# Loads of attention values and compressed keys held back by a one-column write that needs a unit's softmax sum

## The chip, the cores and the metric

The kernel is one program on one core of a Trainium2 chip. The metric is device time in microseconds (us). Before the change the median of 3 runs is 2306.26 us (2304.66 to 2307.88). The profile comes from a further, profiled execution, which took 2301.17 us.

The engines are named as the profile names them: PE (TensorE, matmuls), PEld (its weight loads), DVE (VectorE), ACT (ScalarE), POOL (GpSimd), SP (SyncE, which issues every DMA of this kernel). Each engine works through its instructions in the order in which they stand.

## The reference

The reference is one step of a two-layer encoder on 1024 prompt frames and 64 sample frames, which the kernel handles as 1088 columns of width 1024. Cut to what matters, each layer does this:

```
h = rmsnorm(x);  z = h @ w_in                      # split into the inputs and gates of three mixers
o_a = mla_attend(...) * silu(g_a)                  # 8 heads; keys and values from a compressed ckv
o_b = pool_mix(...) * silu(g_b)                    # trailing means
o_c = ca_attend(...) * silu(g_c)                   # 4 "chunk" heads: own chunk and 8 before it, with a bias
m = gates_a * (o_a @ w_o_mla) + gates_b * (o_b @ w_o_pool) + gates_c * (o_c @ w_o_ca)
x = x + m @ w_out
x = x + sigmoid(rmsnorm(x) @ w_ple_gate) * (ple @ w_ple_proj)
```

For the compressed attention the values of all heads come from one matrix, `v = ckv_all @ w_ukv[:, values]`, where `ckv_all` has 128 features and 1600 columns (1024 prompt, 512 cached, 64 sample).

## The kernel before

Every layer runs as: projections (GEMMs), the attention phase, a merge, the output GEMM, the PLE gate GEMM. Values in float32 are split into a high and a low part (`split`, lines 108 and 119), and products are three matmuls (`mm3`, lines 130 to 132). Large intermediates live in DRAM between the stages.

**Units.** The attention phase (`attn_phase`) takes the 4 chunk heads and then the 8 compressed ("latent") heads one after another. A head has nine units, one for each block of 128 queries; for a chunk head they come in the order `QC` = sample block first, then blocks 0 to 7. Unit i: `scores` on PE with a DVE pass that adds the bias and takes the minimum (chunk heads, L984 and L986), `exp` on ACT (L807), the reciprocal of the sum on DVE (L814), the scaling of the probabilities P on POOL (L815). Two units later they are transposed (pT, L841) and split into PT, and then multiplied by the values V (pv, L867 for the sample block, L875 for a pair of blocks).

**Loads.** `ahead_of` is called by each unit's `scores`: at the second unit of head p it writes the loads of head p+1's Q, K and bias, at the sixth its values (`load_values`). A chunk head's V is one load of 128x1664 (`vc`); there are three V buffers. For the first latent head `values` loads the compressed keys into `ckf` (three pieces: 1024, 512 and 64 columns) and their weights into `wv`, then makes V from them (vps, L1024).

**Background.** Between the units the PLE projection runs (`ple_proj`): 16 steps, each of two blocks of six matmuls (pps), each block copied out of PSUM by ACT (L1394, tile `o`, two buffers), each step stored to DRAM (`pp<-o`). A step can write `o` only when the store of two steps before has landed. `pool_branch` (pu, pa, pb, pbm) and `merge_bc` (wbc, mps, of, g) follow the same manner.

**Order.** The code fixes what depends on what. The order on each engine is then made by the tile layer's scheduler, which places instructions by priority and by its own estimate of when their operands are there (`schedule_with_timeline_sim`). A load whose buffer is free and whose source is written can thus be placed on SP far ahead of its place in the code, and a new dependence moves instructions on every engine. All DMAs are on SP's one hardware queue; a DMA waits on SP for what it depends on and for the completion of an earlier DMA whose semaphore it takes over (there are eight of these), and what is behind it on SP waits with it.

Of the kernel before, what the change touches and what calls it, by code (L numbers as in the profile page):

```python
# [10 lines left out]
F32 = mybir.dt.float32  # L11
# [3 lines left out]
ALU = mybir.AluOpType  # L15
# [8 lines left out]
KT = 1600  # L24
# [49 lines left out]
class K:  # L74
# [382 lines left out]
    def w_pairs(self, l, begin):  # L457
# [129 lines left out]
        def done(k):  # L587
            a, b = z.pop(k), z.pop(k + 1)
            if k == Z_HQ:
                for j, t in enumerate((a, b)):  # L590
                    self.st(zd[k + j], t)
                self.tasks.append(stat(a, b))
            elif k == Z_CKV:
                def dst1(i, t):
                    self.st(d["ckv"][l], t)

                def dst2(i, t):
                    self.st(d["krope"][l], t[64:96])
                    store_hl(t, keydst(self.kr_d[l], slice(0, 32)), slice(64, 96))
                self.tasks.append(norm([a], S_128, 1, G_KV, dst1))  # L600
                self.tasks.append(norm([b], S_QH, 2, G_KR, dst2))
            elif k in (Z_QC, Z_KC):
                for j, t in enumerate((a, b)):
                    def dst(_, t, j=j):
                        if k == Z_KC:
                            self.st(d["cak"][l][j], t)
                            store_hl(t, keydst(self.kc_d[l][j]))
                        else:
                            store_hl(t, [(self.qc_d[l][j, 0], self.qc_d[l][j, 1], slice(0, T))])
                    self.tasks.append(norm([t], S_64, 2, G_CQ if k == Z_QC else G_CK, dst))  # L610
            else:
                for j, t in enumerate((a, b)):
                    if k == Z_VC:
                        self.st(d["cav"][l][j], t)
                        self.tasks.append(values(j, t))
                    else:
                        self.st(zd[k + j], t)
# [178 lines left out]
    def softmax(self, u, s, n, nb, st):  # L796

        nc = self.nc
        if not hasattr(u, "p"):
            u.p = self.sp.tile([128, 1024], F32, tag="P", name="P", bufs=NP)  # L800
        w = n // len(s)
        if nb == 2:
            nc.vector.tensor_tensor(st[:, 0:1], st[:, 0:1], st[:, 1:2], op=ALU.min)

        def exp():
            for c, x in enumerate(s):
                nc.scalar.activation(u.p[:, c * w:c * w + w], x, AF.Exp, bias=st[:, 0:1], scale=-1.0,  # L807
                                     accum_out=st[:, 2 + c:3 + c])
        u.exp = exp

        def norm():
            if len(s) == 2:
                nc.vector.tensor_add(st[:, 2:3], st[:, 2:3], st[:, 3:4])
            nc.vector.reciprocal(st[:, 4:5], st[:, 2:3])  # L814
            nc.gpsimd.tensor_scalar(u.p[:, :n], u.p[:, :n], st[:, 4:5], 1.0, op0=ALU.mult, op1=ALU.mult)  # L815
        u.norm = norm

# [97 lines left out]
    def load_values(self, p):  # L915
        if p < len(self.seq) and self.seq[p] not in self.vt:
            kind, h = self.seq[p]
            if kind == "c":
                v = self.vt[kind, h] = self.new_v().rearrange("p (b c) -> p b c", b=13)
                self.ld(v, self.vc_d[self.l][h])  # L920
            else:
                self.values(self.l, h)

    def new_v(self, dt=F32R):
        return self.sp.tile([128, 1664], dt, tag="V", name="V", bufs=NV)

    def ahead_of(self, p, qb):

        if qb == QC[0] and p == 0:
            self.load_values(0)  # L930
        order = QC if self.seq[p][0] == "c" else QM
        if qb == order[L1]:
            self.load_head(p + 1)
        if qb == order[L2]:
            self.load_values(p + 1)

    def out_of(self, kind, h):

        k = kind, h // 2
        if k not in self.ot:  # L940
            self.ot[k] = self.sp.tile([128, T], F32, tag="o", name="o", bufs=2)
        return self.ot[k]
# [50 lines left out]
    def load_latent(self, h, *t):  # L993
# [6 lines left out]
                self.ld(x[64:96], self.kr_d[l][n - 2])  # L1000
        return t

    def values(self, l, h):

        nc, sp = self.nc, self.sp
        if h == 0:
            self.ckf = self.at("ckf", KT, "ckf", F32)
            self.ld(self.ckf[:, :1024], self.d["ckv"][l][:, :1024])
            self.ld(self.ckf[:, 1024:1536], self.d["ckv_c"][l])
            self.ld(self.ckf[:, 1536:], self.d["ckv"][l][:, 1024:])  # L1010
            self.wv = self.at("wv", 512, "wv", F32)
            self.ld(self.wv, self.d["wukv"][l][:, 512:])
        vs = []
        for i in range(2):
            v = self.new_v().rearrange("p (b c) -> p b c", b=13)
            nc.gpsimd.memset(v[0:64, 12].bitcast(F32), 0.0)
            self.vt["m", h + i] = v
            vs.append(v)
        for b0 in range(0, 13, 4):
            nb = min(4, 13 - b0)  # L1020
            ps = self.pv.tile([128, 4, 128], F32, tag="v", name="vps")
            for b in range(nb):
                c0 = min((b0 + b) * 128, KT - 128)
                nc.tensor.matmul(ps[:, b], lhsT=self.ckf[:, c0:c0 + 128], rhs=self.wv[:, h * 64:(h + 2) * 64],  # L1024
                                 start=True, stop=True)
            p0 = 64 if b0 == 12 else 0
            for i, v in enumerate(vs):
                v = v[p0:, b0:b0 + nb]
                self.split(ps[p0:, :nb, 64 * i:64 * i + 64], v[:, :, :64], v[:, :, 64:])
# [603 lines left out]
```

## Time and profile before

| | |
|---|---|
| median of 3 runs | 2306.26 us |
| profiled execution | 2301.17 us |
| its span | 2299.2 us, 44770 instructions |
| busy share: PE, PEld, DVE, ACT, POOL | 94%, 90%, 80%, 53%, 30% |
| DMA: SP's queue, share of 16 engines' span | 53.9%, 382.95 MB in 221972 packets |
| chain that ended last | PE 63%, DVE 14%, DMA 12%, issue 3%, ACT 3%, POOL 2%, SPq 1% |

PE is busy nearly everywhere. In the page's 40 slices of 57.5 us each the DMA share is highest in the slice from 575 us (9 tenths) and just behind 1725 us, which is where the attention phase of each layer begins; PE's busy digit and its granted clock dip near there too. The phase of the first layer begins at about 560 us and that of the second at about 1700 us.

The time outside the span is 2301.17 - 2299.2 = 1.97 us.

### The profile page before, as it was taken

To read this page: it belongs to the slowest core of one execution; us is meant where nothing else is said; L and a number is where in the kernel's file an instruction comes from. 1 tells how busy PE (TensorE), PEld (TensorE's weight loads), DVE (VectorE), ACT (ScalarE), POOL (GpSimd) and SP (SyncE) were. 2 spreads that over 40 slices of the span, in tenths; PEclk is the share of its full clock that TensorE was granted. 3 is DMA by queue.
4 is the path that set the end of the run, shared out by engine and by line. 5 is a ranking of instruction groups with operands and counts; after the bars stand their busy time and mean duration, and the time that the engine had idled before them with its cause. 6 is when DMAs were issued, how large, how long until landed. Compare 5 with 4: busy or idle time off the path is not lost.

```text
span 2299.2 us, 44770 instructions
## 1 busy us (share of the span) xinstructions
PE 2160.5 (94%) x16134; PEld 2077.4 (90%) x16134; DVE 1838.5 (80%) x3750; ACT 1211.6 (53%) x2549; POOL 694.0 (30%) x918
## 2 busy tenths in 40 slices
PE   5999999999789999998979999999988899999988
PEld 4999999999688999998969999999987789999988
DVE  8677887675678888989997778877746788889898
ACT  6334355554676666445553343555546766654452
POOL 0000044666456553000000001547563565430000
PEclk8999999999899999998979999999999999999989
DMA  3534546355976764454634354544469766645354
GB/s 128 181 110 138 191 147 187 119 157 171 266 203 173 199 170 163 164 193 144 211 105 148 117 170 167 171 142 146 151 178 268 202 179 187 187 156 190 140 160 135
DMA packets 222192, 385.81 MB, mean 168 GB/s; under 512 B 30404, under 2 KB 114196, under 8 KB 221972
## 3 DMA queue, kind: packets, MB, share of 16 engines
q1 hardware_dynamic: 221972, 382.95, 53.9%
q8 instruction: 129, 2.11, 0.4%
q14 instruction: 91, 0.75, 0.1%
HBM read 248.16 MB, written 134.70 MB: 167 GB/s over the span
## 4 chain that ended last, share of the span: by engine, by line
PE 63%; DVE 14%; DMA 12%; issue 3%; ACT 3%; POOL 2%; SPq 1%; POOLq 0%; DVEq 0%; ACTq 0%
PE g L366 41%; PE S L1055 4%; PE pv L875 3%; PE pT L841 3%; DMA pp<-o 3%; DMA K<-bias_p 1%; PE mps L130 1%; DVE wop L119 1%; DMA r<-rd 1%; PE mps L132 1%; PE mps L131 1%; SPq L85 1%; DMA Q<-qc 1%; PE vps L1024 1%; DMA g<-z 1%
## 5 line engine op out<-in xcount | busy, mean ns | idle before, releaser
L108 ACT CAST wop<-wraw 128x512 fp32r<-128x512 f32 (+1 forms) x230 | 139.0, 606 | 266.7 <-PE g L366 180.0
L108 ACT CAST wop<-S 128x512 fp32r<-128x512 f32 x234 | 144.5, 619 | 154.0 <-PE g L366 146.6
L119 DVE TENSOR_TENSOR wop<-S,wop 128x512 fp32r<-128x512 f32 x210 | 163.9, 780 | 66.3 <-ACT wop L108 65.9
L815 POOL TENSOR_SCALAR P<-P,st 128x640 f32<-128x640 f32 (+8 forms) x216 | 156.0, 727 | 200.9 <-DVE st L814 128.6
L119 POOL TENSOR_TENSOR wop<-wraw,wop 128x512 fp32r<-128x512 f32 (+1 forms) x80 | 98.8, 1237 | 381.4 <-ACT wop L108 377.2
L119 DVE TENSOR_TENSOR PT<-pT,PT 128x512 fp32r<-128x512 f32 (+4 forms) x360 | 167.8, 474 | 43.1 <-ACT PT L108 41.1
L366 PE MATMUL g<-B11h,wop 128*128 128x272 f32 x960 | 175.5, 294 | 18.3 <-ACT B11h L110 12.3
L366 PE MATMUL g<-T3h,wop 128*128 128x272 f32 x960 | 178.2, 294 | 12.4 <-ACT T3h L108 11.9
L366 PE MATMUL g<-B21h,wop 128*128 128x272 f32 x960 | 180.6, 299 | 4.2 <-ACT P L378 4.1
L366 PE MATMUL g<-T2h,wop 128*128 128x272 f32 x960 | 177.6, 295 | 5.4 <-ACT T2h L108 5.3
L366 PE MATMUL g<-T1h,wop 128*128 128x272 f32 x960 | 176.1, 295 | 3.5 <-DVE z L629 1.9
L108 ACT CAST PT<-pT 128x512 fp32r<-128x512 f32 (+4 forms) x360 | 147.1, 421 | 54.6 <-PE pT L841 48.2
L366 PE MATMUL g<-T4h,wop 128*128 128x272 f32 x960 | 174.9, 294 | 0.4 <-DVE U L374 0.4
L366 PE MATMUL g<-B22h,wop 128*128 128x272 f32 x960 | 171.5, 289 | 0.0
L875 PE MATMUL pv<-PT,V 128*128 128x256 f32 x928 | 166.7, 299 | 2.1 <-DVE PT L119 1.2
L1055 PE MATMUL S<-K,Q 96*128 96x384 f32 (+5 forms) x672 | 159.7, 354 | 7.8 <-ACT P L807 7.7
L841 PE MATMUL pT<-ident,P 128*128 128x128 f32 x936 | 159.0, 279 | 2.9 <-DVE PT L119 1.5
L366 PEld LDWEIGHTS g<-B11h,wop 128*128 128x128 f32 x960 | 143.1, 192 | 20.3 <-ACT B11h L110 12.9
L130 PE MATMUL mps<-oh,wop 128*128 128x272 f32 x512 | 154.8, 304 | 5.2 <-ACT oh L108 3.1
L366 PEld LDWEIGHTS g<-T3h,wop 128*128 128x128 f32 x960 | 143.9, 192 | 15.4 <-ACT T3h L108 13.6
L366 PEld LDWEIGHTS g<-B21h,wop 128*128 128x128 f32 x960 | 147.2, 197 | 6.5 <-ACT P L378 6.2
L366 PEld LDWEIGHTS g<-T2h,wop 128*128 128x128 f32 x960 | 145.2, 194 | 7.1 <-ACT T2h L108 6.7
(270 smaller groups left out, 6461.5 us busy)
## 6 DMA issues: line engine op xcount, KB each, us to landing
wraw<-win SPq DMA_DIRECT2D x88, 512.0 KB
z<-z SPq DMA_DIRECT2D x96, 272.0 KB
g<-z SPq DMA_DIRECT2D x64, 272.0 KB
z<-z SPq DMA_DIRECT2D x24, 544.0 KB
Q<-q SPq DMA_DIRECT2D x32, 408.0 KB
K<-k SPq DMA_DIRECT2D x32, 400.0 KB
k<-hl SPq DMA_DIRECT2D x48, 256.0 KB
q<-hl SPq DMA_DIRECT2D x64, 192.0 KB
```

What stands on the lines that cost most here:

```text
L85: self.nc.sync.dma_start(out=self.raw(out), in_=self.raw(in_))
L108: nc.scalar.copy(out, src)
L119: e.tensor_sub(out, src, hi)
L130: mm(ps, lhsT=wh, rhs=xh, start=first, stop=False)
L131: mm(ps, lhsT=wh, rhs=xl, start=False, stop=False)
L132: mm(ps, lhsT=wl, rhs=xh, start=False, stop=last)
L366: nc.tensor.matmul(ps[:, c, :C], lhsT=hl[:, w, kb, :], rhs=b[:, kb, c * C:(c + 1) * C], start=k == 0 and not more, stop=k == 11, skip_grou ...
L815: nc.gpsimd.tensor_scalar(u.p[:, :n], u.p[:, :n], st[:, 4:5], 1.0, op0=ALU.mult, op1=ALU.mult)
L841: nc.tensor.transpose(ps[:, j], p[:, c0:c0 + 128], self.ident)
L875: nc.tensor.matmul(ps[:, :w], lhsT=v(b), rhs=grp[b // 4][:, b % 4, j, :w], start=i + j == 0, stop=i == len(bl) - 1 and j == 1)
L1024: nc.tensor.matmul(ps[:, b], lhsT=self.ckf[:, c0:c0 + 128], rhs=self.wv[:, h * 64:(h + 2) * 64], start=True, stop=True)
L1055: nc.tensor.matmul(ps[:, :ww], lhsT=q[0:96, q0:q0 + 128], rhs=k[0:96, k0 + c * w:k0 + c * w + ww], start=i == 0, stop=i == 2 and not diag)
```

## The change

Two things are done. The reciprocal's tile of the unit that was last recorded is kept (`unit_st`), and `after(ap)` writes one column of a tile with it, on POOL. Such a column is written in V's first column before the load of the second, third and fourth chunk head's values, and in columns 0 and 1024 of `ckf` before its first two pieces; the load overwrites it. So none of these five loads can be issued before that write. And the loads of `ckf` and `wv` move out of `values` to the sixth unit of the third chunk head (`load_ckv`), one head earlier in the code. The third piece of `ckf` (64 columns, from column 1536) and `wv` get no such write.

```diff
@@ softmax
             nc.vector.reciprocal(st[:, 4:5], st[:, 2:3])
+            self.unit_st = st
             nc.gpsimd.tensor_scalar(u.p[:, :n], u.p[:, :n], st[:, 4:5], 1.0, op0=ALU.mult, op1=ALU.mult)
@@ load_values
                 v = self.vt[kind, h] = self.new_v().rearrange("p (b c) -> p b c", b=13)
+                if p:
+                    self.after(v[:, 0, 0:1])
                 self.ld(v, self.vc_d[self.l][h])
             else:
                 self.values(self.l, h)
+
+    def after(self, ap):
+
+        self.nc.gpsimd.tensor_scalar(ap, self.unit_st[:, 4:5], 1.0, 1.0, op0=ALU.mult, op1=ALU.mult)
@@ ahead_of
             self.load_values(p + 1)
+            if p == 2:
+                self.load_ckv()
@@
+    def load_ckv(self):
+
+        l = self.l
+        self.ckf = self.at("ckf", KT, "ckf", F32)
+        for c in (0, 1024):
+            self.after(self.ckf[:, c:c + 1])
+        self.ld(self.ckf[:, :1024], self.d["ckv"][l][:, :1024])
+        self.ld(self.ckf[:, 1024:1536], self.d["ckv_c"][l])
+        self.ld(self.ckf[:, 1536:], self.d["ckv"][l][:, 1024:])
+        self.wv = self.at("wv", 512, "wv", F32)
+        self.ld(self.wv, self.d["wukv"][l][:, 512:])
+
     def values(self, l, h):
 
         nc, sp = self.nc, self.sp
-        if h == 0:
-            self.ckf = self.at("ckf", KT, "ckf", F32)
-            self.ld(self.ckf[:, :1024], self.d["ckv"][l][:, :1024])
-            self.ld(self.ckf[:, 1024:1536], self.d["ckv_c"][l])
-            self.ld(self.ckf[:, 1536:], self.d["ckv"][l][:, 1024:])
-            self.wv = self.at("wv", 512, "wv", F32)
-            self.ld(self.wv, self.d["wukv"][l][:, 512:])
```

The unit whose sum is kept at that moment is the fifth of the head (block 3, 512 columns), since the sixth unit's `scores` calls `ahead_of` before its own sum is recorded.

The change moves instructions. Below are three places, first before and then after; a row is a source line, the operation, what it writes and reads, and its shape.

**SP, first layer, behind the bias loads of the second chunk head.** V are values, `ckf` and `wv` the compressed keys and their weights, `pp` the PLE steps' stores, `pu` the pooling branch, Q_7183 (7184 after) the first load of the third chunk head. Before:

```order
L85 DMA K_6887<-bias_s 128x576
L85 DMA V<-vc_125 128x1664 x2
L85 DMA ckf<-ckv 128x1024
L85 DMA ckf<-ckv_c 128x512
L85 DMA ckf<-ckv 128x64
L85 DMA wv<-wukv 128x512
L85 DMA pp_107<-o 128x544 x2
L85 DMA pu<-z_105 128x1024
L85 DMA pu<-hist 128x15
L85 DMA pu<-z_105 128x64
L85 DMA wraw<-wpp 128x2x128
L85 DMA Q_7183<-qc_121 64x1088
```

After:

```order
L85 DMA K_6887<-bias_s 128x576
L85 DMA ckf<-ckv 128x64
L85 DMA wv<-wukv 128x512
L85 DMA pp_107<-o 128x544
L85 DMA pu<-z_105 128x1024
L85 DMA pu<-hist 128x15
L85 DMA pp_107<-o 128x544
L85 DMA pu<-z_105 128x64
L85 DMA wraw<-wpp 128x2x128
L85 DMA V<-vc_125 128x1664
L85 DMA Q_7184<-qc_121 64x1088
```

The V of the second head now stands behind two PLE stores, the pooling input and a weight, right ahead of the third head's loads; the V of the third head and the two large pieces of `ckf` are gone from here. (The third head's V now stands ahead of the fourth head's Q and K, behind two `pp` stores and a `wbc` load.)

**SP, first layer, the loads of the first latent head.** Q_7749 and K_7751 (7758 and 7760 after) are its Q and K, `kr` its rotary keys. Before:

```order
L85 DMA acc<-z_105 128x1088
L85 DMA Q_7749<-q_117 96x1088
L85 DMA Q_7750<-q_117 96x1088
L85 DMA K_7751<-k_119 64x1600
L85 DMA K_7751<-kr_115 32x1600
L85 DMA pp_107<-o 128x544
L85 DMA K_7752<-k_119 64x1600
```

After:

```order
L85 DMA acc<-z_105 128x1088
L85 DMA Q_7758<-q_117 96x1088
L85 DMA Q_7759<-q_117 96x1088
L85 DMA V<-vc_125 128x1664
L85 DMA ckf<-ckv 128x1024
L85 DMA ckf<-ckv_c 128x512
L85 DMA K_7760<-k_119 64x1600
```

The fourth head's V and the two pieces of `ckf` have come in between Q and K of the first latent head.

**ACT, first layer, end of the first chunk head.** P,st is a unit's exponential, PT and ot belong to its product with V, `o<-pps` copies a block of the PLE projection. The first row is in both the exponential of the same unit. Before:

```order
L879 COPY ot<-pv 64x256
L108 CAST PT<-pT 128x4x128
L807 ACTIVATE P,st<-P,st 128x640 x2
L108 CAST PT<-pT 128x4x128
L807 ACTIVATE P,st<-P,st 128x640
L879 COPY ot<-pv 64x256
L108 CAST PT<-pT 128x128
L108 CAST PT<-pT 128x3x128
L807 ACTIVATE P,st<-P,st 128x576
```

After:

```order
L880 COPY ot<-pv 64x256
L108 CAST PT<-pT 128x4x128
L807 ACTIVATE P,st<-P,st 128x640
L1408 COPY o<-pps 128x272
L807 ACTIVATE P,st<-P,st 128x640
L108 CAST PT<-pT 128x4x128
L807 ACTIVATE P,st<-P,st 128x640
L1408 COPY o<-pps 128x272
L108 CAST wop<-wraw 128x256
L880 COPY ot<-pv 64x256
```

Two copies of the PLE projection (the seventh and eighth of 32) now stand among the first head's exponentials; before, they stand ten and fifteen rows further on, in the second head. The blocks of the PLE projection come earlier on PE in the same way.

## Rows read from the trace of the kernel before

**Rows 1.** Stages, first layer (stretch in us; busy us of PE, PEld, DVE, ACT, POOL; clock; DMA share; GB/s)

```profile
560.00:580.00 20.00, 14.01 (x107) 13.26 (x105) 5.23 (x8) 6.21 (x14) 11.71 (x12) 0.91 1.04 284
580.00:600.00 20.00, 15.29 (x85) 12.84 (x86) 15.95 (x58) 14.16 (x35) 8.26 (x16) 0.83 1.01 242
600.00:620.00 20.00, 17.90 (x120) 16.40 (x119) 12.80 (x55) 13.12 (x40) 7.17 (x15) 0.91 0.99 280
620.00:640.00 20.00, 15.44 (x87) 13.88 (x86) 10.31 (x37) 9.73 (x29) 8.43 (x14) 0.83 1.02 260
640.00:660.00 20.00, 18.08 (x131) 16.34 (x130) 15.68 (x54) 15.55 (x45) 16.17 (x23) 1.00 0.70 219
660.00:680.00 20.00, 16.93 (x117) 15.80 (x118) 14.66 (x50) 13.52 (x43) 8.66 (x14) 0.91 0.50 151
```

**Rows 2.** Stages, second layer, same columns

```profile
1700.00:1740.00 40.00, 32.41 (x189) 28.38 (x188) 20.13 (x60) 20.00 (x47) 19.61 (x27) 0.79 1.00 265
1740.00:1780.00 40.00, 32.44 (x209) 28.29 (x210) 25.02 (x100) 23.99 (x74) 16.07 (x29) 0.96 1.00 278
1780.00:1820.00 40.00, 35.25 (x252) 32.47 (x251) 30.19 (x104) 28.91 (x85) 25.66 (x37) 0.96 0.63 184
```

**Rows 3.** PE's waits, 570 to 650 us: total us, times, longest

```profile
PE pps L130 <- ACT o L1394: 5.6, 4, 3.2
```

**Rows 4.** The chain that ended last, both layers: start us, length us, what

```profile
585.72 13.72 DMA K<-bias_p
599.51 8.80 DMA pp<-o
629.89 9.89 DMA pp<-o
654.45 10.68 DMA pp<-o
...
1735.81 11.43 DMA ckf<-ckv_c
```

**Rows 5.** DMAs issued by SP, 560 to 660 us: count, KB each

```profile
V<-vc SPq DMA_DIRECT2D x4, 832.0 KB
...
ckf<-ckv SPq DMA_DIRECT2D x1, 512.0 KB
...
ckf<-ckv_c SPq DMA_DIRECT2D x1, 256.0 KB
```

**Rows 6.** SP's timeline, first layer: start us, us, DMA, count

```profile
590.90 1.57 SPq L85 DMA_DIRECT2D V<-vc  x2
...
621.36 0.33 SPq L85 DMA_DIRECT2D V<-vc  x1
```

**Rows 7.** PE's timeline, first uses and waits (idle before, releaser in brackets)

```profile
614.46 0.64 PE L867 MATMUL pv<-PT,V 128*128 128x128 f32 x4
...
624.93 0.59 PE L130 MATMUL pps<-oh,wop 128*128 128x272 f32 x1 [3.19 <-ACT o L1394]
...
665.65 0.60 PE L130 MATMUL pps<-oh,wop 128*128 128x272 f32 x1 [2.86 <-ACT o L1394]
...
674.66 0.56 PE L867 MATMUL pv<-PT,V 128*128 128x128 f32 x4
...
675.49 0.72 PE L1024 MATMUL vps<-wv,ckf 128*128 128x128 f32 x5
```

**Rows 8.** ACT's timeline: the wait for a landing store

```profile
608.34 0.39 ACT L1394 COPY o<-pps 128x272 f32<-128x272 f32 x1 [1.77 <-DMA pp<-o]
```

**Rows 9.** POOL's timeline: a small scaling, and the fifth unit of three heads

```profile
588.25 0.38 POOL L815 TENSOR_SCALAR P<-P,st 128x128 f32<-128x128 f32 x1 [0.66 <-DVE st L814]
...
593.19 0.69 POOL L815 TENSOR_SCALAR P<-P,st 128x512 f32<-128x512 f32 x1 [1.16 <-DVE st L814]
...
617.26 0.70 POOL L815 TENSOR_SCALAR P<-P,st 128x512 f32<-128x512 f32 x1 [2.25 <-DVE st L814]
...
649.01 0.69 POOL L815 TENSOR_SCALAR P<-P,st 128x512 f32<-128x512 f32 x1
```

## The prediction

> **What bounds the kernel now.** PE is busy 94% of the span, so I first looked for the stretches in which it isn't, and then for what ends its waits there.
>
> The stages at the start of the first layer's attention phase are the place [rows 1]. From 560 to 640 us the DMA engines are busy all the time (share 0.99 to 1.04), while PE is busy 14.0 to 17.9 of each 20 us and its clock falls to 0.83 to 0.91 of full speed, so for part of each stage it runs at 1.2 GHz and not 2.4. From 640 us the DMA share falls to 0.70 and then 0.50. The second layer shows the same: share 1.00 from 1700 to 1780 us, then 0.63 [rows 2]. So some 80 us per layer are bound by DMA, and the reader should see that what follows has room for more transfers.
>
> PE's waits from 570 to 650 us say how the DMA reaches PE: 5.6 us in four waits are for ACT's copy of a PLE block, L1394 [rows 3]. Two of these long waits stand in PE's timeline, 3.19 us before 624.93 and, later, 2.86 us before 665.65 [rows 7]. ACT in turn waits for a store `pp<-o` to land [rows 8]. The chain gives the reason for the store being late: SP stands from 585.72 for 13.72 us behind the bias load, issues the store at 599.51, and that takes 8.80 us to land; later ones take 9.89 and 10.68 us [rows 4]. In the second layer the chain runs through a `ckf` load of 11.43 us [rows 4]. So a 272 KB store is late because of the bytes queued ahead of it, and those are what the change moves.
>
> **What the change moves.** Before, SP issues the values of the second and third chunk head together at 590.90, the pieces of `ckf` behind them, and the fourth head's values at 621.36 [rows 6]. First used are the second head's values at 614.46, the fourth's at 674.66, and `ckf` at 675.49 [rows 7]. They lie ready for 15 to 70 us while the stores, which somebody waits for, stand behind them.
>
> 1. Bytes out of the full stretch. A V is 832 KB, the two held pieces of `ckf` 512 and 256 KB [rows 5]. By the order rows the second head's V is still issued in the stretch, behind two stores, and so is the third's, which now stands ahead of the fourth head's K and Q; they change place with the stores and loads there, but remain. The fourth V and the two `ckf` pieces go behind Q of the first latent head, whose buffers come free only with the third chunk head's last scores, so past 640 us. That is 832 + 512 + 256 = 1600 KB, 1.638 MB per layer. The full stages of the first layer moved 284, 242, 280 and 260 GB/s [rows 1], mean 266.5, which makes 1638 / 266.5 = 6.1 us; the second 265 and 278 [rows 2], mean 271.5, 6.0 us. If the whole stretch is bound by its bytes, it ends 12.2 us earlier in the two layers together. Bounds: nothing, if PE and ACT turn out to be the limit once the stores land earlier, and at most those 12.2 us plus the PE wait at 665.65 in both layers (2 x 2.86), if the stores there are no longer caught behind loads. I take 12.2: the waits on the copies alone come to 5.6 us in the first layer's 80 us and 2.86 us just behind it, and the half clock between 600 and 640 us (mean 0.87, so a quarter of the time at 1.2 GHz) is worth up to another 5 us, so there is that much to give back.
>
> The Trainium skill (DMA: Bandwidth & Descriptors, Specifications) gives a core some 358 GB/s from HBM; by that the same bytes would be worth 4.6 us a layer, and the sum would be 3 us smaller. The stages measured here stay at 242 to 296 GB/s at share 1.0, and their rate is what I use.
>
> 2. The bytes in their new place. They come into 640 to 680 us, where the share is 0.70 and 0.50: 6 + 10 = 16 us of idle engines [rows 1], against 6.1 us. The room is there, but eleven transfers now stand between two `pp` stores there, where six stood, so the store behind them may take longer to land than the 10.68 us of [rows 4]. In exchange, the new ACT order needs that store later in the third and fourth head, since the PLE copies now come earlier. Bounds: 2.86 us a layer better (the wait at 665.65 goes), 6 us a layer worse (the store waits behind all 1.638 MB and PE with it). I take 0: two blocks of the PLE projection are done by then that were not before, which gives the store more time.
>
> Is anything late for its user? The fourth V is wanted at 674.66 and `ckf` at 675.49 [rows 7]; issued at about 650 us they take no longer than the store issued there before, 10.68 us [rows 4], plus their own 6.1, and land by 667. The third V lies ahead of the fourth head's loads, which were issued from 621.36 on [rows 6], and is wanted midway between 614.46 and 674.66, about 644 us, since the two are two heads apart. The second V, issued at some 600 us, has until 614.46. Each has a cover of 5 us or more.
>
> 3. The writes and what they wait for. Five one-column operations per layer on POOL; the nearest row is a scaling of 128 columns, 0.38 us [rows 9], so at most 1.9 us per layer, and not below 0. POOL is busy 7 to 16 of 20 us in these stages [rows 1] and PE waits for other things: cost 0. The write needs the same reciprocal as the scaling that stands just ahead of it on POOL, so POOL doesn't wait longer for it.
>
> What can wait is SP. The fifth unit's scaling of the first head starts at 593.19, of the second at 617.26, of the third at 649.01 [rows 9]. SP comes to the second V at about 600 us, past its write: no hold. It comes to the third V earlier than the 621.36 at which it issued the loads at this place before [rows 6], by up to the 6 us that have gone from the queue, and also stands there for a PLE store and a weight load; the sum comes at about 618 us or, with what ACT now does in between, a little later. So SP is held some 0 to 3.5 us, with the eight loads of the fourth head and two stores behind it, while the engines work off what is queued. I take 1 us a layer. The fourth V stands behind Q of the first latent head, which waits for the end of the third head, 650 us, so past its write: 0.
>
> 4. Everything else in the program is the same work; latent heads, merge and GEMMs are placed a little differently by the scheduler. There PE is busy nearly all the time, so I take 0, with 2 us either way.
>
> **Sum.** -12.2 + 0 + 0 + 2 x 1 = -10.2 us, on the profiled execution 2301.17 - 10.2 = 2291.0. The median of the runs is 5.1 us above the profiled one; the change is the same, so 2306.3 - 10.2 = 2296.
>
> **Rivals.**
>
> A. *The waits only change place, no difference.* The new ACT order sets the seventh and eighth copy among the first head's exponentials, ten rows earlier. There ACT reaches the seventh at about 598 us. The store it needs is issued at 599.51 and lands at 608.3 today [rows 4, 8]; without the 2432 KB ahead of it (V twice, 512, 256) it lands up to 9 us sooner, some 600 to 603 us. So ACT would stand there 2 to 5 us, where today it waited 1.77 us a little later, and the second head's exponentials behind it start later by that. This eats half or more of the 6.1 us a layer; with 1 us for SP and 2 us from the rest the total comes out at -4 to +4: 2302 to 2310, middle 2305. For it: the scheduler's estimate knows nothing of the full queue. Against it: two of the PLE blocks are then done and don't come again.
>
> B. *SP is held by the third V, slower.* ACT's stand of 2 to 5 us (A) delays the second head's fifth unit to 620 to 623 us, while SP is at the third V by about 615. SP then stands 5 to 8 us with ten transfers behind it. It decides from the point at which the queue runs empty, about 4 us after SP stops (some eight transfers in flight). Then 1 to 4 us per layer of DMA time are lost in the stretch that is bound by it, the stores behind it land later than today's 629.89 + 9.89, and with ACT's loss the layer ends up 2 to 5 us worse instead of 6 better: +4 to +10, middle 2313. For it: the sum and the queue come within 3 us of each other. Against it: what is held is what ACT itself waits for last.
>
> The Trainium skill says on this (DMA: Bandwidth & Descriptors, Anatomy of one DMA) that a semaphore wait happens on the issuing sequencer and the DMA engines only consume their queues. By that a held V holds all behind it on SP, as B has it; SP's 13.72 us behind one bias load [rows 4] agree.
>
> C. *It doesn't hold anything.* The write is there before SP comes, every time, and only the order changes: the forecast without the 2 us for SP, 2294, well inside the forecast's range.
>
> **Chances.** Forecast with C 0.62 (own range 2287 to 2301), A 0.23, B 0.15. What a measurement of this kernel tells from no change is about 0.2%, 4.6 us: 2301.7 to 2310.9. Forecast and C lie below; A lies inside but for its edge; B straddles the upper edge. Faster 0.62, same 0.23, slower 0.15. The range takes the low bound 12.2 + 2 x 2.86 = 18 us, 2288, less 1 for the scheduler, and reaches up through A to the lower half of B: 2287 to 2312.
>
> **What will show it.** Right: in the first 80 us of both attention phases the DMA share stays at 1.0 but the stretch ends some 6 us earlier, 640 to 680 rises to 0.8 or more, and PE's waits on L1394 shrink by half. Step 2 is right if `vps` and the fourth V's first product wait for nothing. Step 3 is wrong if SP's waits name POOL's write with more than 3 us. A shows as ACT waiting for `pp<-o` near 600 us at a copy that stands among the first head's exponentials; B as a hole in the DMA share near 620 us. The whole is wrong if PE is as idle as before from 560 to 680 us although the bytes have gone.

## The result and the profile after

The changed kernel is slower: 2325.51 us (2321.57 to 2329.68) against 2305.46 us, ratio 1.0087 [1.0064, 1.011]. The forecast was 2296, its range ended at 2312. The medians differ by 20.1 us, the two profiled executions by 26.7. The profiled execution took 2327.87 us, its span 2326.0 us with 44803 instructions; the DMAs moved the same 382.95 MB. PE's busy share is 93% (94% before), DVE's 79% (80%), ACT's 52% (53%).

The stages at the start of the first layer's attention phase, to be held against [rows 1] (columns as there), and below them some of the same time in stages of 5 us:

```profile
600.00:620.00 20.00, 15.26 (x103) 12.71 (x101) 11.75 (x44) 11.34 (x34) 6.83 (x14) 0.99 1.00 275
620.00:640.00 20.00, 19.38 (x123) 18.65 (x124) 15.53 (x59) 15.15 (x45) 11.07 (x19) 0.83 0.68 178
640.00:660.00 20.00, 16.63 (x114) 15.52 (x113) 12.65 (x46) 13.56 (x38) 16.23 (x24) 0.91 0.77 250
...
615.00:620.00 5.00, 2.01 (x14) 1.62 (x14) 1.51 (x4) 0.36 (x1) 0.97 (x3) 0.98 0.87 264
620.00:625.00 5.00, 4.49 (x18) 4.49 (x19) 3.19 (x15) 3.62 (x11) 1.80 (x4) 0.50 0.15 56
625.00:630.00 5.00, 5.00 (x36) 4.96 (x35) 4.40 (x17) 3.93 (x11) 2.17 (x4) 0.84 0.63 227
...
640.00:645.00 5.00, 2.36 (x13) 1.93 (x12) 2.35 (x8) 1.69 (x6) 4.02 (x6) 0.87 1.06 390
645.00:650.00 5.00, 5.00 (x36) 5.00 (x35) 1.73 (x5) 2.34 (x8) 3.11 (x5) 0.79 0.34 138
```

In stages of 20 us the DMA share seems to leave 1.0 at 620 us, 20 us earlier than before. The finer stages show a hole and not an end: 0.15 and 0.63 from 620 to 630 us, then 0.93 to 1.06 up to 645 us. Before, the share stays near 1.0 to 640 us without a hole. At the hole SP stands between two stores of the PLE projection. The second is issued when ACT's copy that starts at 622.27 has ended, and ACT had before this waited for an earlier store to land (start, us, what; in brackets the idle time before and what ended it):

```profile
615.80 7.21 SPq L85 DMA_DIRECT2D pp<-o  x2
...
620.07 0.39 ACT L1408 COPY o<-pps 128x272 f32<-128x272 f32 x1 [4.71 <-DMA pp<-o]
```

The second layer has such a hole too (0.15 from 1770 to 1775 us). The fourth head's V and the two pieces of `ckf` did go out of the stretch: SP issues them from 655.77 to 656.72 us. But PE's waits for copies of the PLE blocks from 570 to 650 us did not shrink against [rows 3] (5.6 us):

```profile
PE pps L130 <- ACT o L1408: 6.5, 4, 3.3
```

The large loss is elsewhere. These are PE's waits in the first layer from the first product of the background merge (`mps`) to the output GEMM (what waits, for what; us in total, times, longest), first of the kernel before (702 to 957.6 us), then after (705 to 967 us):

```profile
PE mps L130 <- ACT oh L108: 1.9, 1, 1.9
PE S L1055 <- ACT P L807: 1.7, 3, 0.8
PE mps L130 <- DVE g L1374: 1.2, 2, 0.7
PE pT L841 <- DVE PT L119: 0.8, 3, 0.3
```

```profile
PE mps L130 <- DVE g L1388: 3.5, 3, 1.8
PE S L1069 <- ACT P L807: 2.4, 4, 1.2
PE mps L130 <- DVE g L1468: 1.8, 1, 1.8
PE pT L842 <- DVE st L803: 1.8, 1, 1.8
PE pT L842 <- DVE PT L119: 1.5, 4, 0.5
PE pv L876 <- DVE PT L119: 1.1, 2, 0.9
```

L1374 and L1388 are the same line of `merge_bc`, which multiplies a product by its gate. PE and DVE at the end of this phase in the changed kernel (start, us, engine, line, operation; in brackets the idle time before and what ended it):

```profile
913.37 0.29 PE L130 MATMUL mps<-oh,wop 128*128 128x272 f32 x1
...
914.91 0.39 PE L130 MATMUL mps<-oh,wop 128*128 128x272 f32 x1 [0.64 <-DVE g L1388]
```

```profile
914.42 0.44 DVE L1388 TENSOR_TENSOR g<-g,mps 128x272 f32<-128x272 f32 x1
...
925.27 1.35 DVE L1468 TENSOR_TENSOR g<-g,mps 128x544 f32<-128x544 f32 x2 [5.77 <-DMA g<-z]
```

```profile
926.05 0.40 PE L130 MATMUL mps<-oh,wop 128*128 128x272 f32 x1 [1.82 <-DVE g L1468]
```

The last six background products stand behind the last attention product (pv) here. The merge behind them must wait for their DVE pass (0.64 us), and DVE later waits 5.77 us for a gate of the merge. In the kernel before no background product is left behind the last pv, and PE has no wait over 0.2 us from 900 us to the output GEMM. The second layer has waits of the same lines, and the clock falls too. Two of its stages in the changed kernel, and a wait in the first of them:

```profile
1980.00:2000.00 20.00, 17.97 (x119) 16.72 (x118) 12.56 (x37) 10.09 (x30) 6.86 (x9) 0.83 0.35 103
...
2060.00:2080.00 20.00, 16.86 (x126) 15.36 (x125) 12.59 (x29) 7.54 (x20) 6.42 (x8) 1.00 0.24 77
```

```profile
1987.66 0.39 PE L130 MATMUL mps<-oh,wop 128*128 128x272 f32 x1 [2.03 <-DVE g L1388]
```

A mean of 0.83 says that PE ran some 6.8 of these 20 us at 1.2 GHz instead of 2.4, behind a wait of 2.03 us. In the kernel before the granted clock is 1.00 in every 20 us from 1840 to 2100.

I cut both traces at the first product of the merge's background, the first of the merge proper (the 385th `mps` of the layer) and the first of the output GEMM. The background stretch, with the late heads in it, went from 207.1 to 209.7 and from 205.7 to 214.8 us, the merge from 48.6 to 52.1 and from 48.7 to 51.3: 17.9 of the 26.8 us between the two spans.

This cut has a flaw: the first `mps` stands behind the 144th score matmul of the layer before and behind the 155th after, so the stretch begins later in the work of the changed kernel. The first score of the latent heads, the 113th of 512, is a cut that every order shares. From there to the last score the latent heads went from 217.2 to 220.9 and from 215.8 to 226.0 us, from the last score to the merge from 9.4 to 11.0 us in both layers. With the merge that is 23.2 us, while the chunk heads, from the first score to the 113th, went from 110.6 to 107.9 and from 106.2 to 109.5.

The orders of the two programs show where this comes from. Counted on PE, 114 of a layer's 768 `mps` stand ahead of its 272nd score matmul (of 512) before and 96 after; 360 and 354 ahead of the last score. The scheduler places the background 18 products, three blocks of six, later among the latent heads.

### The profile page after: what moved, and what is told of

Read it like the earlier page. It is cut to its first block, busy times and chain, and to the rows that moved or that the text cites. A ratio compares the mean times of both kernels' runs of the same rounds, so it can differ in the third digit from the quotient of the medians.

```text
span 2326.0 us, 44803 instructions
## 1 busy us (share of the span) xinstructions
PE 2173.1 (93%) x16134; PEld 2086.6 (90%) x16134; DVE 1836.9 (79%) x3750; ACT 1212.6 (52%) x2549; POOL 696.9 (30%) x928
## 3 DMA queue, kind: packets, MB, share of 16 engines
q1 hardware_dynamic: 221972, 382.95, 53.4%
## 5 line engine op out<-in xcount | busy, mean ns | idle before, releaser
L816 POOL TENSOR_SCALAR P<-P,st 128x640 f32<-128x640 f32 (+8 forms) x216 | 159.3, 742 | 207.7 <-DVE st L814 105.4
L119 POOL TENSOR_TENSOR wop<-wraw,wop 128x512 fp32r<-128x512 f32 (+1 forms) x80 | 97.8, 1224 | 388.6 <-ACT wop L108 385.8
L366 PE MATMUL g<-T3h,wop 128*128 128x272 f32 x960 | 178.3, 294 | 13.4 <-ACT T3h L108 12.4
L807 ACT ACTIVATE P<-S,st 128x384 f32<-128x384 f32 (+5 forms) x224 | 126.6, 571 | 62.8 <-DVE st L803 50.0
```

The lines of the kernel that those rows point to most:

```text
L119: e.tensor_sub(out, src, hi)
L366: nc.tensor.matmul(ps[:, c, :C], lhsT=hl[:, w, kb, :], rhs=b[:, kb, c * C:(c + 1) * C], start=k == 0 and not more, stop=k == 11, skip_grou ...
```

## The experiments

Three theories. O: the loss comes from the order that the scheduler makes around the new dependence, which puts the merge's background behind. H: the held loads cost it, by late data or by SP standing. R: any new order moves the time, because the one before happens to be good. Each of e1 to e15 was timed in five rounds beside the kernel before, the changed kernel in four runs of each. "Attention" is the time from a layer's first score to its first product of the output GEMM, in one profile; outside these two stretches all profiles take 1529 to 1540 us. "Latent" is the part of it from the first to the last score of the latent heads. "behind" counts `mps` ahead of score 272 and ahead of the last score.

| run | held | mps at 272, last | attention, us | latent, us | ratio [95%] |
|---|---|---|---|---|---|
| before | - | 114, 360 | 385.8 + 380.1 | 217.2 + 215.8 | 1 |
| same again (e5) | - | 114, 360 | 379.1 + 378.3 | 215.6 + 214.1 | 0.9999 [0.9985, 1.0014] |
| changed | all 5 | 96, 354 | 391.9 + 397.8 | 220.9 + 226.0 | 1.0087 [1.0064, 1.011] |
| e1 | all but 4th V | 114, 360 | 387.6 + 383.0 | 215.3 + 214.0 | 1.0042 [1.0029, 1.0056] |
| e2 | 4th V | 102, 354 | 390.8 + 391.9 | 220.1 + 221.6 | 1.0061 [1.0041, 1.008] |
| e3 | ckf | 96, 354 | 392.2 + 389.7 | 221.1 + 221.2 | 1.009 [1.0074, 1.0106] |
| e4 | none, writes made | 114, 360 | 386.1 + 381.6 | 218.6 + 215.2 | 1.0035 [1.0023, 1.0047] |
| e6 | all 5, a unit earlier | 114, 360 | 388.0 + 384.8 | 218.7 + 216.9 | 1.0058 [1.0045, 1.0072] |
| e7 | 4th V, ckf | 78, 324; 96, 354 | 395.4 + 392.2 | 218.3 + 224.4 | 1.0105 [1.009, 1.012] |
| e8 | none | 102, 348 | 398.0 + 391.9 | 220.1 + 217.7 | 1.0084 [1.0071, 1.0098] |
| e9 | all 5, three o | 114, 360 | 376.8 + 376.1 | 215.7 + 214.4 | 0.9974 [0.9962, 0.9986] |
| e10 | none, three o | 120, 354 | 393.1 + 387.9 | 224.9 + 224.6 | 1.008 [1.0067, 1.0093] |
| e11 | none, 3 V less | 114, 360 | 387.2 + 384.8 | 218.8 + 217.0 | 1.005 [1.0037, 1.0062] |
| e12 | none | 114, 366 | 384.5 + 384.9 | 217.4 + 219.3 | 1.001 [0.9994, 1.0027] |
| e13 | none, three o | 114, 360 | 386.8 + 379.3 | 224.7 + 217.6 | 1.0 [0.9986, 1.0014] |
| e14 | none, three o | 114, 360 | 379.0 + 377.7 | 219.8 + 217.8 | 0.997 [0.9956, 0.9983] |
| e15 | all 5, four o | 114, 360 | 378.1 + 376.4 | 224.7 + 223.2 | 0.9957 [0.9943, 0.9972] |

**The same kernel again (e5)**, with only a comment added. 

> The kernel before, unchanged but for a comment: shows what the comparison and a single profile can tell. All theories: ratio 0.998 to 1.002; by how much its profile's times of the heads and stages differ from those of the first profile of the kernel before is the size below which no stage's difference is read.

The ratio tells 0.15%. A single profile tells less: from the layer's first PLE product to the first `mps`, mostly the chunk heads, this one took 126.1 us in the first layer where the first profile took 131.3, and its span was 12.4 us shorter. So a stage's difference of 5 us between two profiles shows nothing about the chunk heads. The latent heads differ by 1.6 and 1.7 us, and the merge is steadier still: 48.6 and 49.4 us.

**Without the fourth V's write (e1).**

```diff
-                if p:
+                if p in (1, 2):
                     self.after(v[:, 0, 0:1])
```

> The change without the write for the fourth chunk head's values: the second and third V and both pieces of ckf are held as in the changed kernel, the fourth V is free. In this kernel's instruction order the merge's background products (mps) stand among the latent heads' scores where they stood before the change (114 of them at score 272 of 512, 360 at the last), not 18 behind (96, 354) as in the changed kernel. Theory O (the late phase is slow because the order puts the merge behind): the loss of 20 us goes and the gain in the chunk heads stays, ratio to before 0.996 to 1.001, last latent head and merge as before (merge 48.4 us in the first layer). Theory H (holding loads costs, by late data or by SP standing): four of five loads are still held, ratio 1.004 to 1.009. Theory R (any new order moves the time by some 10 us either way): anything from 0.995 to 1.009, without relation to the count of mps.

Half of the loss goes with one write of five, and the late part is as O has it: 205.3 and 204.3 us from the first `mps` to the merge, 48.6 us for the merge in both layers. But the ratio is 0.3% above O's range and at the lower edge of H's. Up to the first `mps` the kernel takes 135.3 and 133.9 us, where the kernel before took 131.3 and 129.7 in one profile and 126.1 and 127.9 in the other: holding the second and third V and `ckf` bought nothing there and may have cost some.

**Only the fourth V (e2), only ckf (e3).** In e2 `if p == 3` and ckf loaded in `values` without writes; in e3 no write for V, `load_ckv` as in the change.

> Only the fourth chunk head's values are held; the other four loads and the place of ckf in the code are as before the change. The order puts the merge's products behind by 12 to 18 (102 at score 272, 354 at the last) as in the changed kernel. Theory O: slow nearly as the changed kernel, ratio 1.005 to 1.011, the loss in the last latent heads and the merge, without the gain in the chunk heads. Theory H: one of five loads held, a V that is wanted at 675 us and issued after 650: at most a fifth to a third of the loss, ratio 1.000 to 1.003, and the loss shows at the fourth head's products. Theory R: no relation, 0.995 to 1.009.

> Only the two pieces of ckf are held and moved one head earlier in the code; no V is held. The order has the merge's products behind exactly as in the changed kernel (96 at score 272, 354 at the last). Theory O: ratio 1.005 to 1.011, like the fourth V alone although another load is held. Theory H: if ckf is what comes late, 1.005 to 1.009, else 1.000 to 1.002; the same load is held in the kernel without the fourth V's write, so by H both must show its cost. Theory R: 0.995 to 1.009.

Two different loads give losses of one size (0.61% and 0.90%, intervals that overlap), and each brings a merge of 52.1 to 52.2 us in the first layer and 50.9 to 51.0 in the second. e1 holds the same ckf as e3 and has less than half its loss, so H's reading of e3, that ckf comes late, falls.

**The writes into a scratch column (e4).**

```diff
-                if p:
-                    self.after(v[:, 0, 0:1])
+                for _ in range({0: 0, 1: 1, 2: 1, 3: 3}[p]):
+                    self.after(self.mark)
```

> The same five one-column writes per layer at the same units, but all into a scratch column of their own, so that no load waits for them; ckf loads stand where they stood before. The order has the merge's products as before (114 at score 272, 360 at the last). Theories O and H: ratio 0.999 to 1.001. Theory R: the order changes a little, so up to 0.5% either way.

Nothing is held and the kernel is 0.35% slower. O and H both miss; R has a share.

**All held, one unit earlier (e6).**

```diff
-            self.unit_st = st
+            self.sts = getattr(self, 'sts', []) + [st]
...
-    def after(self, ap):
+    def after(self, ap, k=2):
-        ... self.unit_st[:, 4:5] ...
+        ... self.sts[-k][:, 4:5] ...
```

> All five loads are held as in the changed kernel and ckf's loads stand at the same place, but the writes take the sum of the fourth unit of the head instead of the fifth. Its order has the merge's products where the kernel before has them (114 at score 272, 360 at the last), not 18 behind. Theory O (the order of the merge among the latent heads makes the late phase slow): late heads and merge of both layers as before (first mps to first product of the output GEMM 254 to 257 us), ratio 0.996 to 1.004, well under the changed kernel's 1.0087. Theory H (held loads cost): five of five are held, ratio 1.006 to 1.010. Theory R (any other order costs some 0.4% beside the kernel before): 1.003 to 1.005.

The merge is as before (48.6 and 48.5 us), and PE's only wait over 0.1 us from 903 to 960 us is this:

```profile
PE pT L842 <- DVE PT L119: 0.2, 1, 0.2
```

The ratio lies between O and H, and the stretch from the first `mps` to the GEMM, 260.8 and 259.0 us, is above O's range. Part of that is the cut: here the first `mps` stands behind the 137th score, seven earlier than before. From the first to the last score of the latent heads it is 218.7 and 216.9 us, 1.5 and 1.1 us more than before (3.1 and 2.8 more than e5). Part of the rest is a single place, the start of the merge's background:

```profile
726.65 0.59 PE L130 MATMUL mps<-oh,wop 128*128 128x272 f32 x1 [3.42 <-ACT oh L108]
```

The stage from 720 us has clock 0.83 (0.91 in the kernel before, 1.00 in e5; the wait is under 2 us in both). So holding all five loads doesn't bring the changed kernel's late loss, but this kernel isn't free either.

**The fourth V and ckf (e7)**: `if p == 3`, ckf as in the change. 

> The fourth V and ckf are held, the second and third V are not. Here the order has the merge's products 36 behind in the first layer (78 at score 272, 324 at the last) and 18 behind in the second (96 and 354). Theory O with a dose: the first layer's stretch from the first mps to the output GEMM takes 266 to 272 us (before 255.6, changed 261.8), the second's 260 to 266; ratio 1.009 to 1.015, slower than the changed kernel though it holds less. Theory H: three of five held, 1.003 to 1.007. Theory R: near 1.004.

It has the highest ratio, though it holds less than the changed kernel (their intervals overlap), and the first layer, 36 behind, has its longest attention phase of the kernels that hold loads. The dose isn't linear: 263.0 us from the first `mps` in that layer, below the 266 expected. 36 products are left behind its last pv.

**Behind without holding (e8).**

```diff
-L1, L2 = 1, 5
+L1, L2 = 1, 3
```

> The kernel before with one number changed: the loads of the next head's values are written at the fourth unit of a head and not at the sixth. No load is held by any write, V and ckf come no later than before. Its order has the merge's products 12 to 18 behind (102 at score 272, 336 against 354 at score 500, 348 at the last). Theory O: slow in the late heads and the merge like the changed kernel, 260 to 266 us per layer from the first mps to the output GEMM, ratio 1.005 to 1.011. Theory H: 0.998 to 1.001, nothing is held. Theory R: near 1.004, without 5 us or more in each late phase.

The decisive run. No write, no held load, values written earlier in the code, and the loss has the changed kernel's size; the stretch from the first `mps` is 266.5 and 265.6 us. The same number also moves the products that make the latent heads' values (vps) two units earlier, so e8 shows that an order alone can cost this much, not that it costs at every place what the changed kernel's does. From 909 us to the output GEMM PE has the changed kernel's waits, on the same two lines (L1374 and L1454 here):

```profile
PE mps L130 <- DVE g L1454: 1.5, 1, 1.5
PE mps L130 <- DVE g L1374: 1.2, 2, 0.6
```

**Three buffers for the PLE blocks (e9, on the changed kernel; e10, on the kernel before).**

```diff
-            o = op.tile([128, H], F32, tag="po", name="o", bufs=2)
+            o = op.tile([128, H], F32, tag="po", name="o", bufs=3)
```

> The changed kernel with three buffers instead of two for the PLE blocks (o), so that a step waits for the store of three steps before. All five loads are held; the order has the merge's products where the kernel before has them (114 at score 272, 360 at the last). PE's waits for copies of o (7 to 9 us in each layer's chunk heads, changed kernel) should fall to 3 or less. Theory O: no late loss (254 to 257 us from the first mps to the output GEMM in each layer) and 5 to 10 us gained in the chunk heads, ratio 0.995 to 1.001. Theory R (any other order costs 0.4%): 1.002 to 1.005. Theory H: 1.004 to 1.009, since everything is held.

> The kernel before with three buffers for o, nothing held. The order has the merge's products 6 ahead of the kernel before at score 272 (120) but 12 behind at score 500 (342) and 6 at the last score (354). If the waits for o are what the chunk heads lose by: 5 to 9 us a layer less there. Theory O: the merge pays its 3.6 and 2.4 us for standing behind at the end, the heads little since the merge isn't behind until late; ratio 0.994 to 1.000. Theory R: 1.002 to 1.005.

One edit, opposite signs, and PE's waits for copies of `o` in e9 are 5.5 and 7.5 us (570 to 700 and 1710 to 1830 us), not 3 or less. Its stretch from the first `mps` to the GEMM, 259.5 and 258.3 us, misses O's range as well, since the first `mps` stands behind the 130th score there; by the shared cut its latent heads take 215.7 and 214.4 us, as in the kernel before. In both the chunk heads gain (119.4 and 119.6 us in the first layer to the first `mps`, against 126.1 and 131.3; from the first score to the 113th 103.1 and 104.0, against 105.6 and 110.6). In e10 the order leaves six products behind the last pv, the merge takes 52.2 and 50.4 us, the latent heads 224.9 and 224.6, and all is lost again; being ahead at score 272 didn't save it. O's sign for e10 was wrong because I took the heads' loss as small.

**One V for all chunk heads (e11).** The other three loads are left out.

```diff
-                v = self.vt[kind, h] = self.new_v()...
-                self.ld(v, self.vc_d[self.l][h])
+                if h == 0:
+                    self.v0 = self.new_v()...
+                    self.ld(self.v0, self.vc_d[self.l][h])
+                self.vt[kind, h] = self.v0
```

> The kernel before, but the four chunk heads of a layer all use the first head's values: the loads of the other three (2496 KB, 2.556 MB a layer) are left out, so that the chunk heads 2 to 4 give other outputs. If the bytes at the start of the attention phase bind, as step 1 of the prediction has it, the chunk heads become 2.556 MB / 266.5 GB/s = 9.6 us a layer shorter (from 126 to 131 us to 117 to 122 in the first), ratio 0.990 to 0.995. If the round trip of the PLE stores and ACT's order bind there and not the bytes: 125 to 131 us as before, ratio 0.998 to 1.004. The merge's order is as before, so theory O adds nothing.

126.7 us to the first `mps` in the first layer: nothing clear of the 5 us between two profiles is gained by 2.556 MB less, and the second layer took 128.4. The DMA share falls to 0.15 from 620 to 625 us here too, so the engines had time to spare. (The order moved a little here as well: the first `mps` stands behind the 137th score.) How long ACT waited at its copies for stores to land, from 570 to 700 us, is below (first fence before, second e11, third e9, fourth e15; from 1710 to 1840 us the four read 11.6, 9.2, 7.5 and 1.4). In e5, the unchanged kernel, it is 9.5 and 9.4 us, so two buffers give 9.2 to 12.1 us with or without these bytes; three give 4.3 to 7.5 (e9, e10, e13, e14), four 0.7 and 1.4:

```profile
ACT o L1394 <- DMA pp<-o: 12.1, 4, 4.6
```

```profile
ACT o L1396 <- DMA pp<-o: 12.0, 4, 6.7
```

```profile
ACT o L1408 <- DMA pp<-o: 4.3, 2, 3.0
```

```profile
ACT o L1408 <- DMA pp<-o: 0.7, 1, 0.7
```

**The merge written earlier (e12)**: `BESIDE` 14 to 18. 

> The kernel before with one number changed, so that the merge's background is written four units earlier in the code. The order has the merge's products where they were until score 416, then 6 ahead (318 against 312 at score 460, 366 against 360 at the last). Theory O in the other direction: late heads and merge as before or up to 4 us a layer shorter, ratio 0.997 to 1.001. Theory R: 1.002 to 1.005 as for any other order.

No difference. R's 0.4% for any new order doesn't hold for this one, and six products ahead buy nothing.

**Three buffers and nothing held (e13: e4 with `bufs=3`; e14: the kernel before with `L2` 5 to 6 and `bufs=3`).**

> Three buffers for o, the same writes into a scratch column, nothing held. The merge's products stand as in the kernel before (114 at score 272, 360 at the last). If the holding adds something to the third buffer: slower than the changed kernel with three buffers (0.9974) by 3 us or more, 0.999 to 1.003, and its chunk heads take 122 us or more a layer (119.4 and 121.9 there). If the third buffer does it all: 0.995 to 0.999 and 118 to 122 us.

> Three buffers for o, nothing held and no added write; the loads of the next head's values are written one unit later in the code than in the kernel before, which gives the same places of the merge's products (114 at score 272, 360 at the last). A second kernel of the kind of the run with the scratch column: by the holding 0.999 to 1.003, by the third buffer alone 0.995 to 0.999. Two such kernels that differ by more than 0.3% would say that the rest of the order decides (theory R).

e14 equals e9 without holding anything, so the holding isn't needed for the gain. e13 by itself would have spoken for the holding by the ranges above; e14 speaks against it. e13 and e14 hold nothing, count the same and differ by 0.3%. Between them lie e13's small writes, which cost 0.2 us each, and the order: either can be the 0.3%, and it is the size of what R can explain here.

**Four buffers (e15)**: e9 with `bufs=4`. 

> The changed kernel with four buffers for o, everything held, the merge's products as in the kernel before. If the stores' round trip is what the third buffer hides, the fourth has little left to hide: PE's waits for copies of o from 5.6 and 7.6 us to 4 or less, 2 to 4 us less in the two layers together, ratio 0.995 to 0.998. If it was the order that came with three buffers: 0.999 to 1.005.

The fastest kernel of all, 0.43% under the kernel before and some 1.3% under the changed one (0.9957 / 1.0087). PE's waits for copies of `o` are 1.5 and 2.3 us, within what was expected. Its first stages:

```profile
600.00:620.00 20.00, 19.32 (x141) 17.80 (x140) 15.37 (x62) 14.85 (x47) 9.07 (x17) 1.00 1.02 269
620.00:640.00 20.00, 18.84 (x139) 17.27 (x139) 14.15 (x53) 15.95 (x49) 18.90 (x30) 1.00 1.04 292
```

The DMA engines are full and PE is busy 19 of 20 us at full clock. A part of the gain returns as a new wait when the merge's background starts early, for the split of its operand:

```profile
PE mps L130 <- ACT oh L108: 7.6, 2, 7.3
```

## Why the prediction was wrong

**Step 4 failed, and it set the sign.** "latent heads, merge and GEMMs are placed a little differently by the scheduler. There PE is busy nearly all the time, so I take 0, with 2 us either way." The profile puts 23.2 us there (17.9 by the cut at the first `mps`). I looked at the order where the loads are issued and not in the latent heads, where a count of `mps` against scores would have shown the background 18 products late. That the order does it and not the holding is shown by e8 (a loss of the same size, nothing held), by e1 and e6 (held, merge as before, half and two thirds of the loss), and by e9 and e14, which are equal with all five loads held and with none. All six kernels with 30 or more background products left at the last score lie at 1.0061 to 1.0105 and have merges of 50.2 to 52.2 us; all eleven other profiles have 48.4 to 49.6 us. By the ratio the border is thin, since e6 lies at 1.0058. The merge's share, some 6 us in the two layers, and 3.2 us just before it have a visible mechanism: products behind the last pv, a wait for their DVE pass, a late gate.

For the latent heads, 13.9 us and the larger share, only a loose correlation is shown. From the first `mps` to the merge PE's gaps sum to 11.9 and 11.3 us in the changed kernel against 5.9 and 5.8, with half-clock stages behind the longest waits. By the shared cut the latent heads take 217.7 to 226.0 us in the six kernels that are behind and 214.0 to 219.3 in the others with two buffers. But e13 takes 224.7 us in its first layer and e15 224.7 and 223.2 with nothing behind, so being behind isn't the only thing that costs time there.

**Step 1 failed too (-12.2 us), in both halves.** The fourth V and `ckf` left the full stretch, but the stretch didn't end earlier: it ended at 645 us with a hole from 620 to 630 (before at 640, in e5 at 635). And time doesn't fall with the bytes, as e11 and e15's stages show. What binds there is in good part the loop of the buffers: ACT copies, SP stores, the store lands, ACT may copy again. Its stores took 8.80 to 10.68 us in [rows 4]. From the first score to the 113th every layer takes 105.4 to 115.0 us with two buffers, 101.0 to 104.1 with three, 94.6 and 95.3 with four. The Trainium skill (Trainium Kernel Development and Optimization, Best Practices) advises two buffers to overlap DMA with compute; here this stretch still gains with the fourth. The kernel's time follows only where the order allows: with three buffers the ratio is 0.997 to 1.008, and e15's interval overlaps e9's.

Two readings under this step were wrong. SP did not stand for 13.72 us behind the bias load: that is the time from this load's issue to its landing, in which SP issued other loads, among them the two V of [rows 6]. SP waited for its landing this long (us in total, times, longest; 583 to 602 us):

```profile
SPq L85 <- DMA K<-bias_p: 0.3, 1, 0.3
```

So this row does not agree with a held SP, as the prediction has it. And the view from which [rows 3] is taken has a longer wait than the four that were added up, 5.7 us for ACT's split of the PLE operand (`oh`); it is 5.5 us after the change.

**Step 2** was right in that PE waits neither for the fourth V nor for ckf; the DMA share of the two stages from 640 us rose to 0.77 and 0.69, not to 0.8. **Step 3** was right in size for the writes: SP stood 0.3 us for a write of V in the first layer and not at all in the second, against 2 us forecast, and the ten writes take 186 to 271 ns each.

**The rivals.** A's mechanism was there (ACT at the PLE copies among earlier exponentials: 9.5 us in three waits for stores). But the unchanged kernel has 9.5 us too (e5), so it fits that no gain came and does not explain the loss. B's sign of being true, a hole in the DMA share near 620 us, did come, and SP did stand there for some 6 us; it stood for a PLE copy and not for the write of V. The chunk heads show no loss clear of the 5 us between two profiles, so B had the right sign of the result for a wrong reason. No rival let the far part of the program move.

**Open:** why e1, e4, e6 and e11, whose background isn't behind, are still 0.35 to 0.58% above the kernel before, while e12 and e5 aren't. In e1 the latent heads and the merge are as before, so its loss lies elsewhere, in the chunk heads or outside the attention phase. e13 against e14 says that small writes and order together can make 0.3%. e6's wait for `oh` and its half clock are one such place; the rest I could not assign, since one profile of the same kernel differs from another by as much.

## What to carry to other kernels

Where a scheduler makes the order from its own estimate, a new dependence is a new order everywhere: before taking 0 for the far parts, count there how the background stands against the foreground, in both orders, and look at what is left behind the last foreground product. A DMA share of 1.0 beside a waiting engine doesn't say that bytes bind; see whether the wait is a buffer's round trip, and try a buffer before moving bytes, with its new order timed too. Coarse stages can make a hole look like an end, so look at finer ones. To compare phases of two orders, cut at a place that both share, and not at background work that moves. A forecast of a few tenths of a per cent also needs a null change, one that reorders and holds nothing, to say how far a mere reshuffle goes.

## What the runs showed of the hardware that was not expected

Two executions of the same kernel differ by 5.2 us in the first chunk heads, while the merge differs by 0.7 us at most. And in e15 PE ran at full clock, 18.8 to 19.3 of 20 us busy, beside DMA engines at share 1.02 to 1.04: full DMA engines as in [rows 1] did not by themselves slow it.
